# Forty-eight narrow projection columns computed beside the retention's first head of values, in a two-layer trunk kernel

## The chip, the cores and the metric

The kernel runs on one core of a Trainium2 chip. The metric is the device time of one execution in microseconds (us), and lower is better. The engines are called by the profile's names: PE multiplies matrices (PEld is its weight load, which runs beside the multiplication), DVE is the vector engine, ACT the scalar engine, POOL the general one, and SP issues every DMA of this kernel. TensorE's clock has two levels, 1.2 and 2.4 GHz; the profile gives what was granted as a share of the full one.

## What is computed

Two layers of a hybrid trunk over 256 context tokens and 512 latent tokens, 1024 wide. Each layer projects the modulated tokens `h` by one wide matrix `w_in` whose columns are split among three groups of heads:

```python
h_l = x * (1 + sc_l) + sh_l
h_c = cx * (1 + sc_c) + sh_c
parts_l = jnp.split(h_l @ w_in, in_splits(), axis=-1)
parts_c = jnp.split(h_c @ w_in, in_splits(), axis=-1)
ssd_l, ssd_c = ssd_mixer(parts_c[0:3], parts_l[0:3], ...)       # z 1024, xbc 1536, dt 16 columns
mla_l, mla_c = mla_mixer(parts_c[3:7], parts_l[3:7], ...)       # q 384, kv 256, kr 32, gate 512
ret_l, ret_c = retention_mixer(parts_c[7:11], parts_l[7:11], ...)  # q 256, k 256, v 512, gate 512
```

Two of these parts are narrow: `dt` (16 columns, the step sizes of the state-space scan) and `kr` (32 columns, the shared rotary key of the attention). The retention's values `v` are 512 columns in four heads of 128. The outputs of the three mixers are concatenated, projected back, and normalised with the residual.

## The kernel before

All 768 tokens are held on chip with features on the partitions: `hh[k]` and `hl[k]` (k = 0 to 7) are the 128-feature slices of `h`, as a high and a low part in the format fp32r. Every projection is made of triples (`mm3`, line 145): high by high, high by low and low by high. The weights come from HBM in slots (`wslot`, line 153): one DMA into `wr` (two buffers), a cast on ACT into `wh` and a subtraction on DVE into `wl` (three buffers each). A projection result lies in one of three PSUM buffers, `acc`.

There are two ways of projecting.

**Feature-major** (`proj_many`, line 175): the weights are the stationary operand, 128 output columns wide, and the tokens stream past: 512 latent ones, then 256 of context, for each of 8 slices and 3 terms. A tile of 128 columns costs 24 multiplications with 512 moving columns and 24 with 256. The tile `M_T` with the 48 columns of `kr` and `dt` is made in the same way, with a stationary operand 48 wide.

**Token-major** (`ret_v`, line 669): for the values `v`, 128 tokens are the stationary operand and the weights stream past, 256 columns (two heads) at a time: 2 passes over 6 token chunks with 24 multiplications each. The mean of each head is taken off on the way out (DVE reduces into `vm`, ACT adds it into `stv`), and a DMA stores the chunk (`rv`).

The order of the work comes from a list of steps for each layer:

```python
STEPS = ("dt0 xbc0 ssd0 rk0 rq0 rk1 mod0 ckv0 xbc1 rv0 ssd1 rq1 ckv1 cq0 cq2 rg0 rg1 rg2 cq1 rg3 g1 g0",
         "dt0 xbc0 rk1 ssd0 rk0 xbc1 rv0 ssd1 ckv1 ckv0 cq0 cq1 rg0 rg1 rg2 rg3 cq2 g0 g1 g2 g3")
```

A scheduler turns this into one fixed order for each engine before the run, and mixes independent steps; `high_priority` moves a step ahead. Each engine then works through its own list in order.

In layer 0 the opening (`start`, line 316) makes three projection tiles slice by slice while the modulation is still being computed from DMAs: `M_T`, `B_T` and `B_T + 2`. The next step, `dt0` (`dt_stage`, line 439), copies them out, transposes the 48 rows back to token-major (line 470), and computes from `dt` the decay terms that the scan needs, ending with a store of `cum` that is read back later as `cf`. In layer 1 `dt_stage` first projects three other tiles for the latent tokens alone, then `M_T` and `B_T`. The step `xbc0` (line 559) takes the convolution (`conv`, line 539) of `B_T`, `B_T + 2` and four tiles from `X_T` on, on DVE, with padded copies in three buffers `xpad`. At the very end `ln_turned` (line 1265) writes the second half of the output from buffers `ho`, which share two slots with `hr`.

Of the kernel before, what the change touches and what calls it, by code (L numbers as in the profile page):

```python
# [9 lines left out]
F32 = mybir.dt.float32  # L10
F32R = mybir.dt.float32r
I32 = mybir.dt.int32
AF = mybir.ActivationFunctionType
ALU = mybir.AluOpType
AX = mybir.AxisListType
# [3 lines left out]
KD = 8  # L19
NCTX = 256  # L20
NLAT = 512
T = NCTX + NLAT
NCH = T // 128
# [9 lines left out]
XC = 772  # L33
# [9 lines left out]
Z_T, X_T, B_T, Q_T, KV_T, G_T, RQ_T, RK_T, RG_T, RV_T, M_T, NWIN = (  # L43
    0, 8, 16, 20, 23, 25, 29, 31, 33, 37, 41, 42)
# [44 lines left out]
class Trunk:  # L89
# [225 lines left out]

    def start(self, P):

        tiles = ((M_T, 48), (B_T, 128), (B_T + 2, 128))
        lat = [self.acc.tile([128, 512], F32, tag="acc", name="p0") for _ in tiles]
        cx = [self.ps("cx", "c0", 3) for _ in tiles]  # L320
        ws = []
        for k in range(KD):
            for j in (0, 1) if k == 0 else (k + 1,):
                if j < KD:
                    self.ada(0, (j, j + 8), P)
            self.make_h0(P, k)
            if not ws:
                for t, m in tiles:
                    ws.append([x[:, :8 * m].rearrange("p (k c) -> p k c", k=8)
                               for x in self.wslot(self.A["win"][0, t][:, :8 * m], 8 * m)])  # L330
            for ps, a, b in ((lat, NCTX, T), (cx, 0, NCTX)):
                for p, (hi, lo), (t, m) in zip(ps, ws, tiles):
                    self.mm3(p[:m, 0:b - a], [(hi[:, k, :], lo[:, k, :], self.hh[k][:, a:b], self.hl[k][:, a:b])],
                             k == 0, k == KD - 1)
        self.first = []
        for pl, pc, (t, m) in zip(lat, cx, tiles):
            st = self.sp.tile([128, T], F32, tag="st", name="c0s", bufs=3)
            self.copy(st[:m, 0:NCTX], pc[:m, 0:NCTX])
            self.first.append([(pl[:m], NCTX, T), (st[:m, 0:NCTX], 0, NCTX)])
# [75 lines left out]
    def step(self, s):  # L415

        l, D, ctx, n, i = self.l, self.D, self.ctx, s[:-1], int(s[-1])
        if n == "dt":
            self.dt_stage()
        elif n == "xbc":  # L420
            self.xbc(i)
        elif n == "ssd":
            self.ssd(i)
        elif n == "rv":
            self.ret_v()
        elif n == "mod":
            self.pending = [(0, (j, j + 1)) for j in range(16, 24, 2)] + [(1, (j, j + 1)) for j in range(0, 24, 2)]
        else:
            t = dict(rq=RQ_T, rk=RK_T, ckv=KV_T, cq=Q_T, rg=RG_T, g=G_T)[n]
            self.spill(l, t + i, D[n][i], gate=n in ("rg", "g"), ctx=ctx or n in ("rk", "ckv"))  # L430
# [8 lines left out]
    def dt_stage(self):  # L439
        nc, S, l, D = self.nc, self.S, self.l, self.D  # L440
# [6 lines left out]
            nc.vector.memset(xp[:, 774:776], 0.0)  # L447
        self.cnt = 0
        if l == 0:
            first = self.first  # L450
        else:
            rq0, rq1, pc2 = self.proj_lat(l, (RQ_T, RQ_T + 1, B_T + 2))
            self.store(D["rq"][0], rq0)
            self.store(D["rq"][1], rq1)
            self.padded = {B_T + 2: self.pad(pc2)}
            first = self.proj_many(l, [(M_T, 48), (B_T, 128)]) + [None]
        self.pre = {B_T: first[1], B_T + 2: first[2]}
        ms = S.tile([48, T], F32, tag="u", name="ms", bufs=2)
        for p, a, b in first[0]:
            self.copy(ms[:, a:b], p)  # L460
        if l == 0:
            self.padded = {}
        for t in (B_T, B_T + 2):
            if t not in self.padded:
                self.padded[t] = self.pad(self.pre[t])
        self.load(D["kr"], ms[0:32, :])
        pt = self.ps("tr", "pt", 2)
        ptv = pt[:, 0:288].rearrange("p (c h) -> p c h", c=NCH)
        for c in range(NCH):
            nc.tensor.transpose(ptv[:, c, :], ms[:, c * 128:(c + 1) * 128], self.ident[:48, :48])  # L470
        n = 2 * NCH * 16
        mk = lambda nm: S.tile([128, 2, NCH, 16], F32, name=nm)
        fl = lambda t: t.rearrange("p d c h -> p (d c h)")
        x, e, s, q = mk("dtx"), mk("dte"), mk("dts"), mk("dtq")
        for d in range(2):
            self.tt(x[:, d], ptv[:, :, 32:48],
                    pc[:, P_DT + 16 * d:P_DT + 16 * d + 16].unsqueeze(1).to_broadcast([128, NCH, 16]), ALU.add)
        self.ts(fl(e), fl(x), -1.0, ALU.mult)
        self.tt(fl(e), fl(e), fl(x), ALU.min)
# [19 lines left out]
        h = NCH * 16  # L499
# [17 lines left out]
        for d, m in ((0, self.mf), (1, self.mb)):  # L517
            pa = self.ps("tr", "pa", 2)
            pb = self.ps("tr", "pb", 2)
            for c in range(NCH):  # L520
                o = pa[0:16, c * 128:(c + 1) * 128] if c < 4 else pb[0:16, (c - 4) * 128:(c - 3) * 128]
# [144 lines left out]
        self.load(D["y"][g][:, :, c * 128:(c + 1) * 128].rearrange("t p i -> p t i"), ys)  # L666


    def ret_v(self):
        l = self.l  # L670
        for n in range(2):
            sl = [self.wslot(self.A["win"][l, RV_T + n * 2 + j]) for j in range(2)]
            sl = [(a.rearrange("p (k c) -> p k c", k=4), b.rearrange("p (k c) -> p k c", k=4)) for a, b in sl]
            for c in range(NCH):
                p = self.acc.tile([128, 512], F32, tag="acc", name="pv")
                cs = slice(c * 128, (c + 1) * 128)
                self.mm3(p[:, 0:256], [(self.hh[k][:, cs], self.hl[k][:, cs], sl[k // 4][0][:, k % 4, :],
                                        sl[k // 4][1][:, k % 4, :]) for k in range(KD)])
                with self.tc.high_priority():
                    st = self.sp.tile([128, 256], F32, tag="stv", name="stv", bufs=2)  # L680

                    vm = self.sp.tile([128, 2], F32, tag="vm", name="vm", bufs=2)
                    self.nc.vector.tensor_reduce(vm, p[:, 0:256].rearrange("p (h e) -> p h e", e=128), axis=AX.X,
                                                 op=ALU.add, negate=True)
                    self.ts(vm, vm, 1.0 / 128, ALU.mult)
                    for h in range(2):
                        self.act(st[:, h * 128:h * 128 + 128], p[:, h * 128:h * 128 + 128], AF.Identity,
                                 bias=vm[:, h:h + 1])
                    self.load(self.D["rv"][:, c, n * 256:(n + 1) * 256], st)


    def blocks(self):
# [572 lines left out]
    def ln_turned(self, P, X, a, b, qsum, xsum):  # L1265


        pc = self.pc[self.l]
        k = (b - a) // 128
        dg, lgr, lbr = self.turn  # L1270
        po = {}
        for f in range(2):
            for c in range(k):
                po[c, f] = (self.acc.tile([128, 512], F32, tag="acc", name="pot") if f or c else
                            self.ps("pot", "pot", 1))
                for t in range(4):
                    self.mm(po[c, f][:, t * 128:(t + 1) * 128], X[4 * f + t][:, c * 128:(c + 1) * 128], dg[:, 4 * f + t],
                            t == 0, False, skip_group_check=True)
        with self.tc.high_priority():
            pd = self.ps("plm", "pld", 2)  # L1280
            self.mm(pd[0:1, 0:b - a], self.selD[:, 0:1], xsum)
            nd = P.tile([1, 256], F32, name="nd")
            self.act(nd[:, 0:b - a], pd[0:1, 0:b - a], AF.Copy, scale=-1.0)
            v = self.variance(P, qsum, xsum, k)
            y = self.rpow(P, v, k)
        for f in range(2):
            fs = slice(512 * f, 512 * f + 512)
            for c in range(k):
                self.mm(po[c, f], nd[:, c * 128:(c + 1) * 128], lgr[:, fs], False, True, skip_group_check=True)
                o = P.tile([128, 512], F32, tag="hr", name="ho", bufs=2)  # L1290
                self.stt(o, po[c, f], y[:, c:c + 1], lbr[:, fs], ALU.mult, ALU.add)
                self.load(self.out[1][c * 128:(c + 1) * 128, fs], o)

# [55 lines left out]
def kmajor(w, c):  # L1349

    k = w.shape[0] // 128
    return np.ascontiguousarray(w.reshape(k, 128, c).transpose(1, 0, 2)).reshape(128, k * c)


def pack(inputs):
    f = {k: np.asarray(v) for k, v in inputs.items()}
    o = {}
# [3 lines left out]
    w = f["w_ada"].reshape(L, 8, 128, 24, 128)  # L1361
    o["wada"] = w.transpose(0, 3, 2, 1, 4).reshape(L, 24, 128, 1024)
    win = f["w_in"]
# [4 lines left out]
    W = np.zeros((L, NWIN, 128, 1024), win.dtype)  # L1368
    for l in range(L):
        for i, s in enumerate(starts):  # L1370
            W[l, i] = kmajor(win[l, :, s:s + 128], 128)
        for n in range(2):
            for j in range(2):
                W[l, RV_T + n * 2 + j] = kmajor(win[l, j * 512:(j + 1) * 512, 4272 + n * 256:4272 + (n + 1) * 256], 256)
        m = np.concatenate([win[l, :, 3216:3248], win[l, :, 2560:2576]], 1)
        W[l, M_T, :, :384] = kmajor(m, 48)
    o["win"] = W
    uq = f["mla_w_uq"].reshape(L, 384, 8, 96)
    cols = np.concatenate([uq[..., :64].reshape(L, 384, 512), uq[..., 64:].reshape(L, 384, 256)], -1)
# [59 lines left out]
```

## Time and profile before

| | |
|---|---|
| median of 3 runs | 1487.1 us (1483.25 to 1488.01) |
| the profiled execution's own time | 1483.76 us |
| its span, first to last instruction | 1481.8 us |
| PE busy | 1426.5 us, 96% |
| PEld busy | 1158.2 us, 78% |
| DVE busy | 1076.6 us, 73% |
| ACT busy | 692.6 us, 47% |
| mean granted TensorE clock | 0.987 |

The sums of the prediction are made against the profiled execution, 3.3 us below the median of the runs. A busy PE is not a PE at its peak: the recorded length of a multiplication includes its way through the array, so the distance between the starts of two neighbours tells what one costs in a stream.

### The profile page before, as it was taken

The numbers are of one execution on the slowest core, as the hardware profiler recorded it, in microseconds if no ns is written. First come the engines' busy times: TensorE is split into PE (matmuls) and PEld (weight loads), VectorE is DVE, ScalarE is ACT, GpSimd is POOL, SyncE is SP. The second block draws the span as 40 slices with busy tenths as digits, with TensorE's granted clock in tenths as the row PEclk, the third lists the DMA queues.
The fourth block names the chain that finished last, engine by engine and source line by source line (L and its number), as shares of the span: only waits on it lengthen the run. The fifth ranks groups of instructions, "written<-read, shape, count | busy, mean of one in ns | idle before, by whom it ended". The sixth has DMA issues, their size and how long they took to land. (4 is left out here: it accounts for less than half of the span.)

```text
span 1481.8 us, 23394 instructions
## 1 busy us (share of the span) xinstructions
PE 1426.5 (96%) x8696; PEld 1158.2 (78%) x8696; DVE 1076.6 (73%) x2077; ACT 692.6 (47%) x1377; POOL 25.7 (2%) x35
## 2 busy tenths in 40 slices
PE   6999999999999999999999899999999999989988
PEld 4787789778888888777788778788778887767667
DVE  3599894995486667678645858997776767678846
ACT  2346743662232443477622345565463344347742
POOL 0000000000000001000001000000000000100010
PEclk9999999999999999999999999999999999999999
DMA  8336553457725746624241223353357465562241
GB/s 337 138 99 180 183 168 110 158 184 256 258 72 175 247 154 198 222 82 131 80 170 58 91 88 111 120 148 114 98 168 251 136 199 190 171 205 89 69 141 57
DMA packets 109725, 226.18 MB, mean 153 GB/s; under 512 B 13534, under 2 KB 41310, under 8 KB 109356
## 3 DMA queue, kind: packets, MB, share of 16 engines
q1 hardware_dynamic: 109612, 224.70, 46.5%
q8 instruction: 68, 1.11, 0.3%
q14 instruction: 45, 0.37, 0.1%
HBM read 174.46 MB, written 50.20 MB: 152 GB/s over the span
## 5 line engine op out<-in xcount | busy, mean ns | idle before, releaser
L101 PE MATMUL pj<-hh,wh 128*128 128x512 f32 (+1 forms) x984 | 354.5, 361 | 2.8 <-ACT hh L115 2.4
L101 PE MATMUL pj<-hh,wl 128*128 128x512 f32 (+1 forms) x984 | 353.2, 359 | 0.0
L101 PE MATMUL pj<-hl,wh 128*128 128x512 f32 (+1 forms) x984 | 350.7, 356 | 0.0
L122 ACT CAST wh<-wr 128x1024 fp32r<-128x1024 f32 (+1 forms) x116 | 120.3, 1039 | 208.8 <-PE pj L101 92.2
L101 PEld LDWEIGHTS pj<-hh,wh 128*128 128x128 f32 x984 | 185.1, 188 | 36.0 <-issue 8.9
L101 PEld LDWEIGHTS pj<-hh,wl 128*128 128x128 f32 x984 | 185.0, 188 | 31.2 <-issue 7.0
L101 PEld LDWEIGHTS pj<-hl,wh 128*128 128x128 f32 x984 | 185.2, 188 | 30.5 <-issue 6.4
L104 DVE TENSOR_TENSOR wl<-wr,wh 128x1024 fp32r<-128x1024 f32 (+1 forms) x116 | 141.0, 1216 | 79.6 <-ACT wh L122 78.5
L104 DVE TENSOR_TENSOR pel<-pe,peh 128x512 fp32r<-128x512 f32 (+1 forms) x112 | 71.6, 648 | 37.0 <-ACT peh L115 36.5
L107 DVE SCALAR_TENSOR_TENSOR cv<-xpad,cw,cv 128x772 f32<-128x772 f32 (+1 forms) x96 | 92.2, 993 | 0.2
L115 ACT ACTIVATE pe<-psc 128x512 f32<-128x512 f32 (+1 forms) x112 | 63.7, 569 | 56.4 <-PE psc L101 47.6
L1043 DVE TENSOR_REDUCE nm<-pmx 128x1 fp32r<-128x768 f32 (+1 forms) x80 | 67.6, 845 | 15.7 <-PE pmx L101 14.5
L101 PE MATMUL po<-sh,wh 128*128 128x512 f32 (+1 forms) x192 | 70.0, 367 | 4.2 <-DVE oy L107 4.2
L101 PE MATMUL po<-sl,wh 128*128 128x512 f32 (+1 forms) x192 | 70.1, 366 | 1.9 <-DVE sl L107 1.9
L115 ACT ACTIVATE ce<-cf 64x512 f32<-64x512 f32 (+1 forms) x80 | 46.9, 587 | 50.3 <-DMA cf<-cum 49.5
L101 PE MATMUL po<-sh,wl 128*128 128x512 f32 (+1 forms) x192 | 69.6, 364 | 0.0
L115 ACT ACTIVATE tm<-sf,dt 128x128 f32<-128x128 f32 x160 | 52.5, 390 | 30.4 <-DVE sf L104 30.3
L115 ACT ACTIVATE peh<-psc 128x512 fp32r<-128x512 f32 (+1 forms) x112 | 63.6, 568 | 0.2
L101 PE MATMUL po<-mr,wh 128*128 128x256 f32 (+1 forms) x216 | 55.5, 343 | 3.1 <-DVE la L107 3.1
L115 ACT ACTIVATE arg<-arg,ncb 128x128 f32<-128x128 f32 x160 | 54.9, 393 | 4.1 <-DVE arg L107 3.6
L101 PE MATMUL pv<-wl,hh 128*128 128x256 f32 x192 | 54.0, 281 | 0.7 <-DVE wl L104 0.7
L101 PE MATMUL pv<-wh,hh 128*128 128x256 f32 x192 | 53.7, 280 | 0.0
(337 smaller groups left out, 2952.1 us busy)
## 6 DMA issues: line engine op xcount, KB each, us to landing
wr<-in_win SPq DMA_DIRECT2D x82, 512.0 KB, 3.8
ar<-in_wada SPq DMA_DIRECT2D x48, 512.0 KB, 7.0
cf<-cum SPq DMA_DIRECT2D x80, 256.0 KB, 4.6
wr<-in_wout SPq DMA_DIRECT2D x32, 512.0 KB, 4.3
y<-ys SPq DMA_DIRECT2D x20, 256.0 KB, 2.5
xs<-th SPq DMA_DIRECT2D x16, 256.0 KB, 2.1
x<-in_xT SPq DMA_DIRECT2D x8, 384.0 KB, 8.6
rv<-stv SPq DMA_DIRECT2D x24, 128.0 KB, 3.0
```

The source lines that it names most:

```text
L101: return self.nc.tensor.matmul(out, lhsT=lhsT, rhs=rhs, start=start, stop=stop, **k)
L104: return self.nc.vector.tensor_tensor(out, a, b, op=op)
L107: return self.nc.vector.scalar_tensor_tensor(out, in0=a, scalar=s, in1=b, op0=op0, op1=op1)
L115: return self.nc.scalar.activation(out, in_, f, **k)
L122: self.nc.scalar.copy(hi, raw)
L1043: nc.vector.tensor_reduce(nm[:, i:i + 1], p1[:, 0:n], axis=AX.X, op=ALU.max, negate=True)
```

## The change

The tile `M_T` goes. Its 48 columns are laid behind the 128 columns of the retention's first head, and are computed token-major with it. `ret_v` becomes a function of a part number and is called three times for a layer: part 0 with 128 + 48 = 176 moving columns, inside `dt_stage`; part 1 with 256 and part 2 with 128 columns where `rv0` stands in the list. Each part has 6 chunks of 24 multiplications. The `dt` columns are then token-major already; the 32 `kr` columns are transposed instead. In the opening, the place of `M_T` is taken by `X_T`, a full tile of 128 columns, whose projection in `xbc0` goes. The weights are packed anew on the host. The buffers `ho` get four slots of their own.

```diff
     def start(self, P):
-        tiles = ((M_T, 48), (B_T, 128), (B_T + 2, 128))
+        tiles = ((X_T, 128), (B_T, 128), (B_T + 2, 128))
...
         elif n == "rv":
-            self.ret_v()
+            self.ret_v(1)
+            self.ret_v(2)
...
         if l == 0:
-            first = self.first
+            self.padded = {t: self.pad(p) for t, p in zip((B_T, B_T + 2, X_T), (self.first[1], self.first[2], self.first[0]))}
         else:
...
-            first = self.proj_many(l, [(M_T, 48), (B_T, 128)]) + [None]
-        self.pre = {B_T: first[1], B_T + 2: first[2]}
-        ms = S.tile([48, T], F32, tag="u", name="ms", bufs=2)
-        for p, a, b in first[0]:
-            self.copy(ms[:, a:b], p)
-        if l == 0:
-            self.padded = {}
-        for t in (B_T, B_T + 2):
-            if t not in self.padded:
-                self.padded[t] = self.pad(self.pre[t])
-        self.load(D["kr"], ms[0:32, :])
-        pt = self.ps("tr", "pt", 2)
-        ptv = pt[:, 0:288].rearrange("p (c h) -> p c h", c=NCH)
-        for c in range(NCH):
-            nc.tensor.transpose(ptv[:, c, :], ms[:, c * 128:(c + 1) * 128], self.ident[:48, :48])
+
+        mt = S.tile([128, XC], F32, tag="u", name="mt", bufs=2)[:, 0:NCH * 48].rearrange("p (c m) -> p c m", c=NCH)
+        self.ret_v(0, mt)
+        if l:
+            self.padded[B_T] = self.pad(self.proj(l, B_T))
+        kt = S.tile([32, T], F32, tag="u", name="kt", bufs=2)
+        for a, b in ((2, 6), (0, 2)):
+            pt = self.ps("tr", "pt", 2)
+            for c in range(a, b):
+                nc.tensor.transpose(pt[0:32, (c - a) * 128:(c - a + 1) * 128], mt[:, c, 0:32], self.ident)
+            self.copy(kt[:, a * 128:b * 128], pt[0:32, 0:(b - a) * 128])
+        self.load(D["kr"], kt)
...
-            self.tt(x[:, d], ptv[:, :, 32:48],
+            self.tt(x[:, d], mt[:, :, 32:48],
...
-    def ret_v(self):
+    def ret_v(self, n, mt=None):
+
         l = self.l
-        for n in range(2):
-            sl = [self.wslot(self.A["win"][l, RV_T + n * 2 + j]) for j in range(2)]
...
+        h0, nh = ((0, 1), (1, 2), (3, 1))[n]
+        w = 128 * nh + (48 if n == 0 else 0)
+        if n < 2:
+            sl = [self.wslot(self.A["win"][l, RV_T + 2 * n + j][:, 0:4 * w], 4 * w) for j in range(2)]
+            sl = [[x[:, 0:4 * w].rearrange("p (k c) -> p k c", k=4) for x in y] for y in sl]
+        else:
+            x = [y.rearrange("p (k c) -> p k c", k=8) for y in self.wslot(self.A["win"][l, M_T])]
+            sl = [[y[:, 0:4] for y in x], [y[:, 4:8] for y in x]]
+        for c in (2, 3, 4, 5, 0, 1):
+            p = self.acc.tile([128, 512], F32, tag="acc", name="pv")
+            cs = slice(c * 128, (c + 1) * 128)
+            self.mm3(p[:, 0:w], [(self.hh[k][:, cs], self.hl[k][:, cs], sl[k // 4][0][:, k % 4, :],
+                                  sl[k // 4][1][:, k % 4, :]) for k in range(KD)])
+            with self.tc.high_priority():
+                if n == 0:
+                    self.copy(mt[:, c], p[:, 128:176])
...
+                self.load(self.D["rv"][:, c, h0 * 128:(h0 + nh) * 128], st[:, 0:128 * nh])
...
-                o = P.tile([128, 512], F32, tag="hr", name="ho", bufs=2)
+                o = P.tile([128, 512], F32, tag="ho", name="ho", bufs=4)
```

## Rows read from the trace of the kernel before

**Rows 1.** The page: busy time, share of the span and instructions of each engine.
```profile
PE 1426.5 (96%) x8696; PEld 1158.2 (78%) x8696; DVE 1076.6 (73%) x2077; ACT 692.6 (47%) x1377; POOL 25.7 (2%) x35
```

**Rows 2.** Busy time by stretch: stretch, length, engines with counts, clock, DMA.
```profile
core 0: us, PE busy (x) PEld busy (x) DVE busy (x) ACT busy (x) POOL busy (x), PEclk, DMA share, GB/s
20.00:40.00 20.00, 18.45 (x194) 13.31 (x194) 9.30 (x19) 4.13 (x7) 0.00 (x0) 1.00 1.02 405
...
58.00:70.00 12.00, 11.62 (x59) 9.83 (x59) 10.31 (x23) 4.15 (x6) 0.00 (x0) 0.86 0.45 141
...
90.00:222.00 132.00, 130.70 (x883) 106.96 (x883) 124.84 (x242) 79.83 (x190) 0.00 (x0) 1.00 0.52 163
222.00:270.00 48.00, 45.57 (x349) 42.17 (x348) 26.90 (x52) 18.99 (x46) 0.00 (x0) 1.00 0.36 114
...
1010.00:1050.00 40.00, 38.46 (x315) 37.13 (x315) 24.89 (x46) 19.84 (x44) 0.00 (x0) 1.00 0.36 116
```

**Rows 3.** One tile's stretch: multiplications into `pv`, columns PE, PEld, DVE, ACT.
```profile
1034.00:1046.00 12.00, 12.00 (x104) 12.00 (x103) 2.01 (x5) 3.13 (x10) 1.00 0.43 138
```

**Rows 4.** Timeline of PE, layer 1, `M_T`: start, length, engine, instruction.
```profile
860.47 0.39 PE L101 MATMUL pj<-hh,wh 128*48 128x512 f32 x1
...
865.08 0.39 PE L101 MATMUL pj<-hh,wl 128*48 128x512 f32 x1
...
870.90 0.28 PE L101 MATMUL pj<-hh,wh 128*48 128x256 f32 x1
...
873.59 0.28 PE L101 MATMUL pj<-hh,wl 128*48 128x256 f32 x1
```

**Rows 5.** Groups by shape, PE: rows*columns of weights, moving shape, count | busy, mean ns.
```profile
L101 PE MATMUL pv<-wh,hh 128*128 128x256 f32 x192 | 53.7, 280 | 0.0
...
L580 PE MATMUL ptr<-K,th 128*128 128x128 f32 x96 | 13.4, 276 | 3.7 <-DVE th L107 3.6
...
L101 PE MATMUL pnm<-identr,nm 128*1 128x128 f32 x80 | 8.7, 222 | 2.3 <-ACT bqh L118 1.6 <-DVE nm L1043 0.5
...
L470 PE MATMUL pt<-K,ms 48*128 48x48 f32 x12 | 1.1, 228 | 1.6 <-ACT ms L118 1.6
```

**Rows 6.** Timeline: a run of four `pnm` multiplications.
```profile
608.64 0.40 PE L101 MATMUL pnm<-identr,nm 128*1 128x128 f32 x4 [1.47 <-ACT bqh L118]
```

**Rows 7.** Groups by shape, PEld: weight loads of 128, 48 and 1 columns.
```profile
L101 PEld LDWEIGHTS pv<-wl,hh 128*128 128x128 f32 x192 | 36.1, 188 | 0.9 <-DVE wl L104 0.9
...
L101 PEld LDWEIGHTS prc<-ones,rsq 128*128 128x128 f32 x80 | 9.7, 191 | 1.0 <-ACT rsq L115 0.3
...
L101 PEld LDWEIGHTS pnm<-identr,nm 128*1 128x1 f32 x80 | 5.1, 82 | 6.6 <-ACT bqh L118 3.2 <-DVE nm L1043 0.7 <-issue 0.7
...
L101 PEld LDWEIGHTS pj<-hl,wh 128*48 128x48 f32 x16 | 1.9, 121 | 0.9
```

**Rows 8.** Timeline of PEld: weight loads for multiplications with one moving column.
```profile
433.62 0.97 PEld L101 LDWEIGHTS prc<-ones,rsq 128*128 128x128 f32 x8
...
448.12 1.90 PEld L101 LDWEIGHTS prc<-ones,rsq 128*128 128x128 f32 x16
```

**Rows 9.** Timeline: the weights' low part on DVE in the opening.
```profile
14.59 0.55 DVE L104 TENSOR_TENSOR wl<-wr,wh 128x384 fp32r<-128x384 f32 x1
...
16.52 1.23 DVE L104 TENSOR_TENSOR wl<-wr,wh 128x1024 fp32r<-128x1024 f32 x1
```

**Rows 10.** Timeline: PE behind the opening.
```profile
57.85 0.57 PE L470 MATMUL pt<-K,ms 48*128 48x48 f32 x6 [1.60 <-ACT ms L118]
...
60.35 0.63 PE L101 MATMUL pj<-hl,wh 128*128 128x512 f32 x1
```

**Rows 11.** Groups by shape, DVE: the reduction of a chunk of `pv`.
```profile
L683 DVE TENSOR_REDUCE vm<-pv 128x2 f32<-128x256 f32 x24 | 10.1, 422 | 22.6 <-PE pv L101 22.4
```

**Rows 12.** Timeline: the last two output pieces.
```profile
1477.15 1.56 DVE L107 SCALAR_TENSOR_TENSOR ho<-pot,rp_y,lbr 128x512 f32<-128x512 f32 x2 [1.33 <-DMA out<-ho]
```

More of the change, by code (lines that the diff above doesn't have):

```diff
@@ L666, in ssd_y @@
         self.load(D["y"][g][:, :, c * 128:(c + 1) * 128].rearrange("t p i -> p t i"), ys)
-    def ret_v(self):
+    def ret_v(self, n, mt=None):
         l = self.l
-        for n in range(2):
-            sl = [self.wslot(self.A["win"][l, RV_T + n * 2 + j]) for j in range(2)]
[L673 to L689, printed above, removed]
@@ new lines, in ret_v @@
+        h0, nh = ((0, 1), (1, 2), (3, 1))[n]
[14 more added lines that the diff above has]
+                    self.copy(mt[:, c], p[:, 128:176])
+                st = self.sp.tile([128, 256], F32, tag="stv", name="stv", bufs=2)
+                vm = self.sp.tile([128, 2], F32, tag="vm", name="vm", bufs=2)
+                self.nc.vector.tensor_reduce(vm[:, 0:nh], p[:, 0:128 * nh].rearrange("p (h e) -> p h e", e=128),
+                                             axis=AX.X, op=ALU.add, negate=True)
+                self.ts(vm[:, 0:nh], vm[:, 0:nh], 1.0 / 128, ALU.mult)
+                for h in range(nh):
+                    self.act(st[:, h * 128:h * 128 + 128], p[:, h * 128:h * 128 + 128], AF.Identity,
+                             bias=vm[:, h:h + 1])
+                self.load(self.D["rv"][:, c, h0 * 128:(h0 + nh) * 128], st[:, 0:128 * nh])
@@ L1371, in pack @@
             W[l, i] = kmajor(win[l, :, s:s + 128], 128)
[L1372 to L1376, printed above, removed]
+        v = win[l, :, 4272:4784]
+        m = np.concatenate([v[:, 0:128], win[l, :, 3216:3248], win[l, :, 2560:2576]], 1)
+        for j in range(2):
+            W[l, RV_T + j, :, :704] = kmajor(m[j * 512:(j + 1) * 512], 176)
+            W[l, RV_T + 2 + j] = kmajor(v[j * 512:(j + 1) * 512, 128:384], 256)
+        W[l, M_T] = kmajor(v[:, 384:512], 128)
     o["win"] = W
```

## The prediction, made before the changed kernel had run

> **What bounds the kernel now.** I read the page first. PE is busy for 96% of the span, the next engine, DVE, for 73% [rows 1]: what counts is how long PE's list is, unless the change opens a hole in it. Then the busy time by stretch. Behind the opening, from 90 to 222 us, PE (130.7 of 132 us) and DVE (124.8) are both nearly full; in the two stretches that hold the values' projection, 222 to 270 and 1010 to 1050, DVE has room (26.9 of 48 us, 24.9 of 40) and PE loses 2.4 and 1.5 us [rows 2]. So PE sets the time there too, and a longer list of PE moves the end by about as much.
>
> The third reading is the pace, because a recorded length (280 ns for 256 columns, 222 for 128) holds the way through the array as well [rows 5]. In a stream of `pv`, 104 multiplications of 256 columns take 12.00 us, one in 115.4 ns [rows 3]. In `M_T`, 512 columns follow each other in 4.61 us over 20 steps, 230.5 ns, and 256 columns in 2.69 us over 23 steps, 117 ns [rows 4]. That is 0.45 ns a moving column, whether the weights are 48 or 128 wide.
>
> **The term that decides: 176 and 128 moving columns.** No fp32r multiplication of this kernel has a stationary operand of 128 columns and fewer than 256 moving ones, so its cost must be bounded. Two things could set the pace: the moving columns, or the load of the next weights.
>
> From below, the moving columns. `pnm` is fp32r with 128 moving columns and a stationary operand of one column: four take 0.40 us, so (0.40 - 0.222) / 3 = 59 ns each [rows 5, 6]. The narrow format therefore pays no penalty of its own at 128 columns, and 176 would be 81 ns in proportion.
>
> From above, the load. A load of 1, 48 and 128 columns is recorded with 82, 121 and 188 ns [rows 7]. From 1 to 128 columns that is 106 ns more, 0.83 ns a column, and the 48 lie on the same line (82 + 39 = 121): 82 ns of delay, then 107 ns in which 128 columns go in. If the array takes in one set of weights at a time, two such loads can't start within 107 ns. The trace has one place that shows this: `prc`, weights of 128 columns with one moving column. Eight loads take 0.97 us and sixteen 1.90 us, so (0.97 - 0.191) / 7 = 111 ns and (1.90 - 0.191) / 15 = 114 ns a step [rows 7, 8], with next to nothing to stream. `pnm`, with one column of weights, shows that PE can step in 59 ns, so the 111 ns are those of the load.
>
> With 256 moving columns the load hides behind the stream (107 under 115). With 176 or 128 it would stand out, and both would cost some 112 ns, almost as much as 256. I take 112 (between the 111 and 114 of `prc`, whose loads are almost as long as those of `pv`, 191 and 188 ns); the bounds are 107 and 117 if the load binds, and 59 and 81 ns if it doesn't.
>
> The sum for a layer. Before: 288 multiplications of `pv` at 0.1154 = 33.2 us, and for `M_T` 24 at 0.2305 and 24 at 0.117 = 8.3 us; 41.6 us together. After: 3 parts of 144; part 1 at 0.1154 = 16.6 us, parts 0 and 2 at 0.112 = 32.3 us; 48.9 us. That is 7.3 us more a layer, **+14.6 us** for both; +11.7 at 107 ns, +17.4 at 117, and -9.6 if only columns count (16.6 + 144 x (0.059 + 0.081) = 36.8 us a layer). In columns the change saves 11,520 of 92,160 a layer, but it issues 432 multiplications for 336, and each brings a load.
>
> The Trainium skill (TensorE: Matmul & The Clock Gate, "Back-to-back issue gap") speaks for the change: it gives a sustained 81 ns for a pair of load and multiplication at 128 columns and 131 ns at 512. The second doesn't agree with this trace, which has 230 ns at 512 columns. By 81 ns for both narrow kinds the sum would be 23.3 + 16.6 = 39.9 us a layer, 3.4 us less in all, where my 112 ns gives 14.6 more.
>
> **The other parts.**
> - Projection of `X_T` in the opening instead of in `xbc0`: the same 48 multiplications with the same moving columns. The weight slot grows from 384 to 1024 columns, which is 320 KB more in a stretch where the DMA engines are full at 405 GB/s [rows 2]: at most 0.8 us. On DVE its low part takes 1.23 instead of 0.55 us [rows 9], before PE's first products. I take +0.5 us, between 0 and 1.
> - Transposes: 12 of the kind of `pt` (228 ns) become 12 with 128 moving columns, like `ptr` (276 ns) [rows 5]: 12 x 0.048 = +0.6 us, at least 0.
> - The pass out of PSUM: 18 chunks a layer are reduced instead of 12, at no more than 0.42 us each [rows 11], with six more small scalings, copies and stores of `rv` on DVE, ACT and SP. For parts 1 and 2 DVE's room in [rows 2] hides it, and with 3 PSUM buffers at 24 x 112 ns = 2.7 us a chunk PE has 5 us before it would miss a buffer. Without that cover, 6 x 0.42 = 2.5 us a layer would stand on the path. I take 0. SP gets 6 more issues a layer; behind them stand weight loads that have a slot of slack.
> - The chain from `dt` to `cum`: in layer 0 it now waits for part 0, some 16 us of PE, instead of standing right behind the opening. What is late is `cum`, and behind it `cf` and the scan. The scan also needs the four convolved tiles of `X`, though, and DVE can begin on three convolutions while PE makes part 0. In layer 1 part 0 (16 us) stands where `M_T` and `B_T` stood (together some 16 us), so `dt` is no later and `B_T` comes 8 us later.
> - The hole behind the opening: PE waits 1.6 us for copies of `ms`, and works on at half pace (0.63 instead of 0.40 us recorded) under a granted clock of 0.86 [rows 2, 10]. The next weights are cast behind the same number of copies on ACT, so this hole stays, without the wait for the transposes. With convolutions begun earlier, some of the 2.4 and 1.5 us of [rows 2] may go as well. I take -1.2 us, bounds -5 and +3.
> - Four slots for `ho`: DVE waited 1.33 us for a store before the third piece [rows 12], but that piece also needs PE's last products. I take -0.5 us, between -1.3 and 0.
>
> Sum: 14.6 + 0.5 + 0.6 - 1.2 - 0.5 = **+14.0 us**. The profiled execution's 1483.8 becomes 1497.8; beside the median of the runs, 3.3 us above it, this is 1501.
>
> **The rivals.**
> 1. *The load doesn't bind.* If two loads may run side by side in this form, the moving columns count: -9.6 + 0.5 + 0.6 - 1.2 - 0.5 = -10.2 us, 1477. (The Trainium skill's page named above would have it at 81 ns: -3.4 - 0.6 us, 1483.) For it: the 48-wide and 128-wide weights show the same pace at 256 columns, so no load has been seen to cost there. Against it: `prc`. It decides as soon as the narrow pace is under some 87 ns, where 288 x pace + 16.6 us equals the 41.6 us of before.
> 2. *The holes pay for it.* The load binds at its lower bound, +11.7, and the holes behind the opening and in the values' stretches close altogether, some 8 us, with the earlier convolutions: about +3 us, 1490, not to be told from no change. Against it: DVE has no room from 90 to 222 us, and what it gains there must first be met by PE's work.
> 3. *The late chain hurts as well.* `cum` comes 16 us later in layer 0 and the tiles of `X` 8 us later in layer 1; if the scan waits for either, PE runs out of other work, and 5 to 8 us come on top: 1508. Against it: PE has the other projections of the list to fill in.
>
> **How the numbers follow.** The forecast, a load-bound pace and slower by 9 to 20 us, gets 0.72; rival 1 0.15; rival 2 0.08; rival 3 0.05. About 0.3% (4.5 us) is what the runs can tell from no change. Faster: rival 1 in most of its reach and a little of rival 2, 0.16. Same: most of rival 2 and the edge of rival 1, 0.09. Slower: 0.75. The forecast's own range is 1494 to 1508. The 8-in-10 range takes in rivals 2 and 3 and the slower edge of rival 1: 1483 to 1511.
>
> **What would show it.** In the changed kernel's rows: the distance between starts in `pv` with 176 and 128 columns, 107 to 117 ns if I am right, near 81 and 59 if rival 1 is; the busy time of PE, up by about 14 us, with PEld nearly as full as PE in the three parts; PE's idle time behind the opening still near 2 us; `dt`'s first operation in layer 0 some 16 us later, and DVE busy with `cv` before it. I am wrong if the narrow multiplications step faster than some 87 ns, or if PE's idle time, not its list, moved the end.

## The result, and the profile after

The changed kernel takes 1521.6 us in the median (1521.2 to 1525.2) against 1485.8 for the kernel before in the same comparison: 1.0246, 95% interval 1.0222 to 1.0269, or 36 us more. The prediction was slower by 14 us, within 1483 to 1511: the sign was right, the size well below half. The span grew from 1481.8 to 1519.5 us. The page's row of the engines, beside [rows 1], and its row of the granted clock in 40 slices:

```profile
PE 1460.7 (96%) x8888; PEld 1193.8 (79%) x8888; DVE 1081.0 (71%) x2101; ACT 694.2 (46%) x1389; POOL 25.7 (2%) x35
...
PEclk9779999999999999999999899999999999999999
```

PE is busy for 34.2 us more and idle for 3.5 us more: its busy time grew, as forecast, but more than twice as much. How much of that is a longer list, and how much the clock, is worked out below. Two slices near the start stand at 7, where no slice of the kernel before was under 9. Three stretches of `pv` show why (as in [rows 2], and to be read beside the pace of [rows 3]): part 0 of layer 0, part 0 of layer 1, part 2 of layer 1.

```profile
62.00:88.00 26.00, 26.00 (x124) 26.00 (x124) 3.36 (x11) 3.87 (x11) 0.00 (x0) 0.50 0.20 66
893.00:905.00 12.00, 12.00 (x110) 12.00 (x109) 5.12 (x26) 4.81 (x14) 0.00 (x0) 1.00 0.41 133
1075.00:1088.00 13.00, 13.00 (x119) 13.00 (x118) 3.25 (x12) 2.35 (x7) 0.00 (x0) 1.00 0.39 118
```

Where the clock is 1.00 (2.4 GHz), 12.00 us hold 110 multiplications and 13.00 us hold 119: 109 ns each, with PEld as full as PE. In layer 0 the granted clock is 0.50 (1.2 GHz) for the whole stretch, and 26.00 us hold only 124: 210 ns. DVE, moreover, does next to nothing there, 3.36 of 26 us. The timeline of PE, for the way into part 0 of layer 0, the way out of it, and the pace in layer 1:

```profile
57.06 0.28 PE L101 MATMUL c<-hh,wl 128*128 128x256 f32 x1
59.34 0.57 PE L101 MATMUL pv<-wh,hh 128*128 128x176 f32 x3 [2.00 <-ACT wh L122]
60.26 0.52 PE L101 MATMUL pv<-wl,hh 128*128 128x176 f32 x1 [0.35 <-DVE wl L104]
...
75.51 0.41 PE L101 MATMUL pv<-wh,hl 128*128 128x176 f32 x1
...
80.63 0.41 PE L101 MATMUL pv<-wh,hl 128*128 128x176 f32 x1
...
91.58 0.78 PE L101 MATMUL pj<-hh,wh 128*128 128x512 f32 x1
...
93.43 0.63 PE L101 MATMUL pj<-hl,wh 128*128 128x512 f32 x1
93.86 0.45 PE L101 MATMUL pj<-hh,wl 128*128 128x512 f32 x1
94.15 0.39 PE L101 MATMUL pj<-hh,wh 128*128 128x512 f32 x1
...
891.50 0.28 PE L101 MATMUL pv<-wh,hh 128*128 128x176 f32 x1
...
897.64 0.28 PE L101 MATMUL pv<-wh,hl 128*128 128x176 f32 x1
```

The last two rows are 55 steps apart: 6.14 / 55 = 111.6 ns. In layer 0 the recorded length goes from 0.28 to 0.41 us behind a hole of 2.00 and 0.35 us, and the rows of 75.51 and 80.63 are 24 steps apart: 5.12 / 24 = 213 ns. It stays so until the projections with 512 moving columns: the one at 93.43 still takes 0.63, the one at 94.15 0.39. In [rows 2, 10] the same fall was made good sooner: a clock of 0.86 over 12 us is 3.4 us at the half level, and such projections stood right behind the hole. Last, DVE: `dt`'s first operation, the first convolution, and the last two output pieces, and behind them the first two of these in the kernel before:

```profile
91.12 0.25 DVE L104 TENSOR_TENSOR dtx<-mt,pc 128x96 f32<-128x96 f32 x1
...
106.65 0.68 DVE L112 TENSOR_SCALAR cv<-xpad,cw 128x772 f32<-128x772 f32 x1 [1.83 <-DMA cum<-ct]
...
1514.11 0.75 DVE L107 SCALAR_TENSOR_TENSOR ho<-pot,rp_y,lbr 128x512 f32<-128x512 f32 x1
1515.82 0.75 DVE L107 SCALAR_TENSOR_TENSOR ho<-pot,rp_y,lbr 128x512 f32<-128x512 f32 x1 [0.96 <-PE pot L101]
```

```profile
58.46 0.42 DVE L104 TENSOR_TENSOR dtx<-pt,pc 128x96 f32<-128x96 f32 x2 [4.66 <-PE pt L470]
...
75.79 0.69 DVE L112 TENSOR_SCALAR cv<-xpad,cw 128x772 f32<-128x772 f32 x1 [2.02 <-ACT ct L118]
```

No convolution runs under part 0. The first one stands behind the whole chain of `dt` and waits at its end for the transfer of `ct`, whose buffers (tag `cv`) are those of the convolutions. In the kernel before it stands in the same place, 31 us earlier.

### The profile page after: what moved, and what is told of

The parts are those of the page before. It is cut to its first block, busy times and chain, and to the rows that moved or that the text cites. A ratio compares the mean times of both kernels' runs of the same rounds, so it can differ in the third digit from the quotient of the medians.

```text
span 1519.5 us, 23852 instructions
## 1 busy us (share of the span) xinstructions
PE 1460.7 (96%) x8888; PEld 1193.8 (79%) x8888; DVE 1081.0 (71%) x2101; ACT 694.2 (46%) x1389; POOL 25.7 (2%) x35
## 5 line engine op out<-in xcount | busy, mean ns | idle before, releaser
L101 PE MATMUL pj<-hh,wh 128*128 128x512 f32 (+1 forms) x952 | 342.0, 360 | 4.2 <-ACT hh L115 2.4
L101 PE MATMUL pj<-hl,wh 128*128 128x512 f32 (+1 forms) x952 | 342.6, 360 | 0.0
L101 PE MATMUL pj<-hh,wl 128*128 128x512 f32 (+1 forms) x952 | 340.8, 358 | 0.0
L101 PEld LDWEIGHTS pj<-hh,wh 128*128 128x128 f32 x952 | 180.1, 189 | 36.0 <-issue 7.9
L101 PEld LDWEIGHTS pj<-hl,wh 128*128 128x128 f32 x952 | 180.2, 189 | 29.8 <-issue 7.2
L101 PEld LDWEIGHTS pj<-hh,wl 128*128 128x128 f32 x952 | 180.3, 189 | 28.7 <-issue 6.1
L101 PE MATMUL pv<-wh,hh 128*128 128x176 f32 (+2 forms) x288 | 86.0, 300 | 2.1 <-ACT wh L122 2.0
L101 PE MATMUL pv<-wl,hh 128*128 128x176 f32 (+2 forms) x288 | 86.4, 300 | 0.4 <-DVE wl L104 0.4
L101 PE MATMUL pv<-wh,hl 128*128 128x176 f32 (+2 forms) x288 | 86.5, 300 | 0.0
L101 PEld LDWEIGHTS pv<-wh,hh 128*128 128x128 f32 x288 | 61.1, 213 | 3.1 <-ACT wh L122 2.6
```

The source lines that it names most:

```text
L101: return self.nc.tensor.matmul(out, lhsT=lhsT, rhs=rhs, start=start, stop=stop, **k)
```

## The experiments

Three accounts were to be told apart. **Pace and clock:** the load holds narrow multiplications at 112 ns (+14.6 us), and in layer 0 part 0 also runs at half the clock: 144 x (213 - 111.6) ns = +14.6 us. **Late chain:** what comes late on DVE costs the time, whatever the clock. **Pace alone** would leave 20 us without a cause. Ratios are to the kernel before; a difference of 0.001 is 1.5 us.

### A. The load's price by itself: `split3` and `split3b`

Both cut one of the two passes of values of the kernel *before* into two of 128 columns, in both layers; nothing else changes. `split3` cuts the first pass of `rv0`:

```
+            for h0, nh in ((0, 1), (1, 1)) if n == 0 else ((0, 2),):      # split3b: n == 1
+                for c in range(NCH):
...
+                    ws = slice(h0 * 128, (h0 + nh) * 128)
+                    self.mm3(p[:, 0:128 * nh], [(self.hh[k][:, cs], self.hl[k][:, cs], sl[k // 4][0][:, k % 4, ws],
+                                                 sl[k // 4][1][:, k % 4, ws]) for k in range(KD)])
...
```

> The kernel before, with only the first pass of ret_v cut into two passes of one head (128 columns): 432 multiplications a layer for 288, the same columns in all, M_T and the opening untouched. It runs in the stretch of rv0, where PE has the full clock. If the load of 128 weight columns binds (111.5 ns a step at 128 columns): 288 x 0.1115 + 144 x 0.1154 = 48.7 us a layer for 33.2, so +15.5 us a layer and about +31 us in all, with 111 to 112 ns between starts. If only the columns count (59 ns at 128 columns): the time stays within 0.3%. If the +36 us of the changed kernel come from the late chain to cum and an idle VectorE rather than from the pace: also near no change, since dt and cum stand where they stood.

Measured: 1.0622 (1.0588 to 1.0655), +93 us, three times the expectation. Windows of `pv` (columns PE alone), and the timeline of PE: the hole, and the change from 128 to 256 columns:

```profile
core 0: us, PE busy (x), PEclk, DMA share, GB/s
255.00:285.00 30.00, 30.00 (x143) 0.50 0.05 14
290.00:295.00 5.00, 5.00 (x29) 0.60 0.63 224
295.00:300.00 5.00, 5.00 (x45) 1.00 0.15 52
```

```profile
234.18 1.54 PE L580 MATMUL ptr<-K,th 128*128 128x128 f32 x6 [6.40 <-DVE th L107]
...
288.96 0.41 PE L101 MATMUL pv<-wh,hl 128*128 128x128 f32 x1
289.17 0.52 PE L101 MATMUL pv<-wh,hh 128*128 128x256 f32 x1
...
293.76 0.41 PE L101 MATMUL pv<-wh,hh 128*128 128x256 f32 x1
293.97 0.32 PE L101 MATMUL pv<-wl,hh 128*128 128x256 f32 x1
294.13 0.28 PE L101 MATMUL pv<-wh,hl 128*128 128x256 f32 x1
```

PE waited 6.40 us for a convolution soon after the pass began, the clock fell, and 30 us in which PE was never idle show 0.50 and 210 ns a step. The pass of 256 columns that follows without a gap starts at 0.21 us a step as well, and from 293.97 on, 4.8 us later, runs at the full level. So what brought the level back was the wider stream. The second layer repeats it, with 3.5 us. `split3b` has the same multiplications with the wide pass first:

> split3 with the other pass of the values cut: the pass of 256 columns goes first in rv0, so that the convolutions' waits fall into it, and the 288 multiplications of 128 columns follow it without a hole. If a hole and narrow columns together are needed to keep the clock low: granted clock 1.00 in the narrow stretch, 111 to 112 ns a step, +15.5 us a layer, so about +31 us on the kernel before (1519) and some 60 less than split3. If a long load-bound stream lowers the clock by itself: again some 210 ns a step and near 1580.

Measured: 1.0237 (1.0198 to 1.0277), +35 us. Windows of `pv`: the hole's place, just behind it (both in the wide pass), and the narrow stretch:

```profile
235.00:240.00 5.00, 4.07 (x21) 0.66 0.37 131
240.00:244.00 4.00, 4.00 (x36) 1.00 0.11 36
252.00:272.00 20.00, 20.00 (x182) 1.00 0.14 45
```

In layer 0 the clock fell here too, but in the wide pass, which brought it back; in layer 1 it didn't fall. The narrow stretch then steps in 20.00 / 182 = 110 ns, and holds the full level for as long as it lasts. The price is confirmed (31 expected, 35 with an interval of 29 to 41). That it is the load which sets it, and not another limit of each multiplication with 128 weight columns, still rests on `pnm` and `prc` [rows 6, 8], since no run changed the weights' width. The 58 us between the two kernels are the order of the passes, with the hole that falls into one or the other.

### B. The clock in part 0: `warm` and `pad256`

`warm` takes the step `rk0` of layer 0 (512 and 256 columns) out of `STEPS[0]` and puts it ahead of part 0; `pad256` fills part 0 with 80 columns of zeros, in both layers:

```
+        if l == 0:
+            self.step("rk0")
         self.ret_v(0, mt)
...                                   # above warm, below pad256
-        w = 128 * nh + (48 if n == 0 else 0)
+        w = 256 if n == 0 else 128 * nh
```

> The changed kernel, with the projection rk0 (48 multiplications of 512 and 256 columns) of layer 0 moved ahead of part 0. Theory 1 (part 0 of layer 0 ran at the 1.2 GHz level because nothing with wide columns stood between the hole behind the opening and it): the granted clock in part 0 is near 1.00, its steps some 112 ns instead of 213, and the kernel gets some 15 us faster than the changed one, about 1506 us. Rival (the chain from dt to cum, late by part 0, starves the scan): dt comes as late or later, the kernel stays at 1520 or gets up to 8 us slower, whatever the clock.

> The changed kernel, with part 0 padded from 176 to 256 moving columns by 80 columns of zeros (both layers); number of multiplications, loads and order stay. At full clock that costs 144 x (0.1154 - 0.1116) = 0.5 us a layer. If it is the narrow columns that leave the clock at 1.2 GHz behind the opening, the clock comes back early in part 0 of layer 0 and the kernel is some 10 to 15 us faster than the changed one (1507 to 1512). If the load-bound stream as such doesn't bring the clock back, or the hole ahead of it sets the clock, part 0 stays at some 210 ns a step and the time is 1521 to 1523.

Measured: `warm` 1.0120 (1.0094 to 1.0147), `pad256` 1.0138 (1.0116 to 1.0160), 19 and 16 us under the changed kernel's 1.0246. Windows of `pv` in part 0 of layer 0, of `warm` and then of `pad256`:

```profile
66.00:80.00 14.00, 12.50 (x113) 12.62 (x113) 1.17 (x4) 2.27 (x8) 1.00 0.31 106
```

```profile
60.00:74.00 14.00, 14.00 (x122) 14.00 (x121) 1.46 (x5) 2.84 (x10) 1.00 0.41 129
```

Both are at 1.00, with 111 and 115 ns. Columns of zeros, which compute nothing, made the kernel 16 us faster. In both a part 0 that is shorter also lets `dt` begin earlier (84.7 and 76.5 us for 91.12), and in `pad256` PE then waits 4.08 us for an `xpad` buffer at 98.8, 1.77 in the changed kernel, so the gains hold other things as well; what the clock costs by itself is in the steps, 213 for 111 ns. "No gain", the rival's word for `warm`, is out. But in both the level never fell behind the opening, and a 256-column pass in the same place did see it fall (`late`, below). So these two runs price the level; that a wider stream brings it back is shown by `split3` and `late`.

### C. The late chain: `late`, `ahead`, `ahead2`

`late` moves, in the kernel before, the first pass of values of layer 0 (256 columns) to the place of part 0:

```
+        if l == 0:
+            self.ret_v((0,))
...
         pt = self.ps("tr", "pt", 2)
...                                   # rv0 of layer 0 keeps the second pass alone
```

> The kernel before with its first pass of values (256 moving columns, 144 multiplications) in layer 0 moved from rv0 to the place of part 0: behind the opening, ahead of the transposes of ms, so ahead of dt. Same instructions, only their order. If the late chain from dt to cum costs time of its own beside pace and clock: dt's first operation in layer 0 some 17 us later, the first pst that much later, and at the end of layer 0 and of the program 5 to 9 us more than before. If the lateness is made up by PE's other projections, as the prediction had it: within 0.3% of before.

Measured: 1.0019 (1.0004 to 1.0033), +2.8 us: inside the 0.3% of the second branch, with an interval that just passes it. The six transposes of `ms` kept their place ahead of the pass, so `dt` began at 58.94 and only what comes behind PE's next step was late: the first convolution at 88.13 against 75.79. The run prices 12 us of lateness, not the 31 us of the changed kernel.

The same run is the plainest control for the clock. In the place of part 0, with waits of PE of 1.60, 0.38 and 0.58 us in front, it has 144 multiplications of 256 columns. The level fell, with steps of 0.21 us, and came back under these multiplications some 7 us later; 176 columns in that place didn't bring it back in 31 us:

```profile
60.00:70.00 10.00, 9.45 (x57) 9.46 (x58) 7.28 (x17) 2.51 (x7) 0.00 (x0) 0.67 0.45 130
70.00:80.00 10.00, 10.00 (x88) 10.00 (x87) 4.66 (x16) 3.15 (x9) 0.00 (x0) 1.00 0.26 95
```

`ahead` is the changed kernel with the convolutions of B and C of layer 0 in front of part 0; `ahead2` has them in `ret_v(0)`, behind the casts of its weights:

```
+        self.cw = ...              # both: cw, uB and uC move here from further down
...
         self.ret_v(0, mt)          # ahead: conv(B_T), conv(B_T + 2) in front of this line
...
         for c in (2, 3, 4, 5, 0, 1):
+            # ahead2: in front of this loop, if n == 0 and l == 0
+            self.conv(B_T, self.uB)
+            self.conv(B_T + 2, self.uC)
```

> The changed kernel, with the two convolutions of B and C of layer 0 put ahead of part 0 in DVE's order (ct no longer ahead of them in the buffers of cv). If DVE's idle time under part 0 (25 of 32 us) is what the late chain costs: 6 to 9 us faster than the changed kernel, 1513 to 1516, with the granted clock in part 0 still near 0.50 and some 213 ns a step. If DVE's idle time is free, or if the reductions of part 0 behind the convolutions hold PE up for buffers: 1520 or more.

> ahead again, with the two convolutions of layer 0 behind the casts of part 0's weights, so that PE doesn't wait 5.6 us for them between 60 and 70 us. Part 0 still runs at the 1.2 GHz level, and DVE convolves under it. If the late convolutions are a part of the 36 us of the changed kernel: 6 to 9 us faster than it, 1513 to 1516. If they are not: within 0.3% of it, 1517 to 1526.

Measured: `ahead` 1.0231 (1.0216 to 1.0245), `ahead2` 1.0174 (1.0142 to 1.0207). One window, 60 to 70 us, of `ahead` and then of `ahead2`:

```profile
60.00:70.00 10.00, 4.39 (x20) 4.39 (x21) 9.13 (x11) 2.74 (x3) 0.00 (x0) 0.50 0.23 74
```

```profile
60.00:70.00 10.00, 10.00 (x49) 10.00 (x49) 9.13 (x12) 3.19 (x6) 0.00 (x0) 0.50 0.48 165
```

DVE is busy for 9.13 us in both, mostly with convolutions. In `ahead` the low parts of the weights stood behind those convolutions on DVE, and PE lost 5.6 us in the window; what was gained was given back. Without that hole the new order is worth 0.0072, some 11 us (5 to 17 with both intervals; 9.1 by the spans), at an unchanged clock of 0.50 in part 0. So the order of the convolutions costs something. How much isn't shown. The page of `ahead2` has

```profile
PE 1451.4 (96%) x8888; PEld 1189.1 (79%) x8888; DVE 1081.1 (72%) x2101; ACT 695.4 (46%) x1389; POOL 25.7 (2%) x35
```

and PE's timeline in the changed kernel, where the late convolutions hold it up:

```profile
112.70 0.38 PE L101 MATMUL pj<-hh,wh 128*128 128x256 f32 x1 [1.77 <-ACT xpad L118]
```

PE is idle for 59.0 of 1510.4 us in `ahead2`, and for 58.8 of 1519.5 in the changed kernel. The wait of 1.77 us is gone, but all of the 9.1 us lie in its busy time, with the same 8888 multiplications. Some 2 us of them come from the opening, ahead of every convolution (PE is busy for 37.33 us from 15 to 57 us, at a clock of 1.00; 39.48 at 0.96 in the changed kernel). The mean granted clock of the whole is 0.980 for 0.976: some 12 us less at the half level, or 6 us of time (an estimate from these two numbers), the opening included. What lowered the clock at the other places, and whether the late convolutions had a part in it, is open. Whether the order on DVE or the buffers shared with `ct` made them late wasn't separated.

### D. Fewer loads: `wide2` and what follows from it

Values and the 48 columns in two passes instead of three, 304 and 256 columns, so 288 multiplications a layer:

```
-        h0, nh = ((0, 1), (1, 2), (3, 1))[n]
+        h0, nh = ((0, 2), (2, 2))[n]
```

> The changed kernel, with the values and the 48 columns in two passes instead of three: 304 columns (two heads and the 48) and 256 columns, 288 multiplications a layer, in the places of part 0 and of rv0. At the full clock 144 x (304 x 0.45 + 115.4) ns = 36.4 us a layer against 48.9 for the three parts and 41.6 for the kernel before. If the pace of the load is what the three parts cost, the kernel is some 25 us faster than the changed one, or 40 if the clock comes back as well: 1481 to 1496. Rival (the late chain to cum sets the +36): part 0 at 304 columns ends later than at 176, and the time stays above 1510.

> wide2 with the projection rk0 of layer 0 ahead of the pass of 304 columns. If the 2.4 GHz level through the opening's end is worth something and the later dt isn't: 2 to 4 us under wide2, 1484 to 1487. If each us that dt is later comes back as a wait for DVE's convolutions: no gain or up to 5 us slower.

Measured: 1.0001 (0.9982 to 1.0019), 36 us under the changed kernel, and 1.0000 (0.9984 to 1.0016) with `rk0` in front, no gain. In `wide2` the fall behind the opening is made good inside the part (0.50 at 62 to 64 us, 1.00 at 66 to 78). Against the kernel before, 10 us should have been won. The timeline of PE in `wide2` has a part of the loss:

```profile
102.03 0.40 PE L101 MATMUL pj<-hh,wl 128*128 128x512 f32 x1
106.91 0.58 PE L101 MATMUL pj<-hh,wh 128*128 128x256 f32 x1 [4.49 <-ACT xpad L118]
```

`pj` has to leave PSUM for an `xpad`, of which there are three, and these are held by convolutions that haven't been made. Three kernels move the convolutions, in both layers (in layer 1 the projection of B goes ahead of the pass too): `wide2_conv` as in `ahead`, `wide2_c2` as in `ahead2`, `wide2_c1` with B's alone.

> wide2 (passes of 304 and 256 columns) with the convolutions of B and C put ahead of the first pass in DVE's order, in both layers; in layer 1 the projection of B goes ahead of the pass as well. wide2 should have gained 10 us on the kernel before by its multiplications and gained none. If the idle DVE took those 10 us: 5 to 10 us faster than before, 1477 to 1482. If not: within 0.3% of wide2, or slower where the reductions behind the convolutions hold up PE's buffers.

> wide2_conv with the two convolutions put behind the casts of the pass's weights instead of ahead of them, so that the hole of 6.4 us of PE that wide2_conv opened at 60 to 70 us closes and DVE still convolves under the first pass. If late convolutions are what ate wide2's 10 us: the wait of PE for xpad at 102 us (4.49 us in wide2) is gone and the time is 1478 to 1484, faster than before by 0.3 to 0.7%. If the 10 us go elsewhere: within 0.3% of before again.

> As wide2_c2, with the convolution of B alone under the first pass, so that the reductions of the pass stand behind 5.7 us of DVE less. If DVE's convolutions hold up the reductions and so PE's three buffers in wide2_c2, this is the faster of the two, by 1 to 3 us; if only the amount of DVE work done under the pass counts, it is 2 to 4 us slower than wide2_c2.

Measured: `wide2_conv` 1.0002 (0.9991 to 1.0014), `wide2_c2` 0.9961 (0.9947 to 0.9976), `wide2_c1` 0.9945 (0.9929 to 0.9962). Windows of `wide2_conv`, then two of `wide2_c2`:

```profile
60.00:70.00 10.00, 3.64 (x13) 3.35 (x14) 10.00 (x12) 2.39 (x3) 0.00 (x0) 0.50 0.10 31
```

```profile
60.00:70.00 10.00, 9.36 (x50) 9.04 (x49) 8.17 (x10) 1.61 (x4) 0.00 (x0) 0.69 0.47 138
...
100.00:110.00 10.00, 10.00 (x57) 8.55 (x57) 8.59 (x10) 5.10 (x10) 0.00 (x0) 1.00 0.45 111
```

`wide2_conv` only moved the hole forward (6.4 us lost at 60 to 70). With the casts first, PE is full from 100 to 110 and the kernel is 6 us faster than the one before, 8 us with B's convolution alone. These two beat both kernels. Which of them is better isn't told by intervals that overlap. Here the late convolutions do show as a wait: PE's idle time over the whole span is 66.0 us in `wide2` (in an execution 4 us above its median), 60.1 in `wide2_c2` and 58.7 in `wide2_c1`.

## Why the prediction was too small

- **The term that decides** held at the full clock: 111.6 ns at 176 columns and 112 at 128 (six steps in 0.67 us at 1075.5), where 112 was taken from `prc` [rows 7, 8]; rival 1 with 59 and 81 ns is out. Its 14.6 us are in the 36. The rule of the Trainium skill that the prediction weighed (TensorE: Matmul & The Clock Gate, "Back-to-back issue gap", 81 ns at 128 columns) doesn't agree with these rows.
- **The step that failed** is part 0 of layer 0 in that sum: "parts 0 and 2 at 0.112" was applied to a place where the prediction itself had read a granted clock of 0.86 and half pace behind the hole. It said that "this hole stays", and took its price to stay as well. The hole stayed (2.35 us for 1.60), but what stood behind it changed, from 512 moving columns to 176, and the half level lasted over 30 us instead of 3.4. That is the missing 14.6 us: 213 instead of 111.6 ns for 144 multiplications; `warm` and `pad256` won back as much and a little more, with `dt` earlier too.
- **The second step that failed:** "DVE can begin on three convolutions while PE makes part 0". It began on none: 106.65 us instead of 75.79, and `dt` at 91.12 instead of 58.46, twice as late as forecast, because part 0 took twice as long. The listing could have told: in `dt_stage` `ct` takes both buffers of the tag `cv` ahead of the first convolution. `ahead2` puts at most some 11 us on this, and the trace of the changed kernel shows only 1.77 us of it as a wait of PE. Rival 3 had the right direction (5 to 8 us on top), but by the wait for `cum`; what the run moved were the convolutions.
- **Opening** +0.5: the last product of the opening ends some 1.1 us later (59.34 - 2.00 against 57.85 - 1.60 of [rows 10]), but that is the clock and not the larger slot: the two rows below are the same opening in the changed kernel and in `pad256`, where PE needs 2.2 us less at 1.00 for 0.96 and ends at 55.2. So the term itself came out at nothing or below. **`ho`** -0.5: the wait of 1.33 us for the store [rows 12] is gone, 0.96 us for PE's last products took its place; right. **Holes** -1.2: wrong in sign, since PE's idle time grew by 3.5 us in all. Rival 2 falls with it.

```profile
15.00:57.00 42.00, 39.48 (x347) 31.09 (x348) 19.57 (x48) 12.00 (x21) 0.00 (x0) 0.96 0.66 253
```

```profile
15.00:57.00 42.00, 37.24 (x348) 29.71 (x348) 19.62 (x48) 13.98 (x26) 0.00 (x0) 1.00 0.69 261
```

The 37.7 us between the spans can be divided without the experiments. The granted clock stands at 0.50 or at 1.00, so a mean of 0.976 over 1519.5 us is some 73 us at the half level, and 0.987 over 1481.8 us some 39. The 34 us more cost about 17 us, if PE is busy in them (an estimate): 14.6 in part 0, the rest in the opening and in places that weren't looked into. That leaves 17 of the 34.2 us of busy time for a longer list, where the prediction had 14.6 + 0.5 + 0.6, and 3.5 us are PE's idle time. So the load and the clock of part 0 carry 29 of 37.7, and the late convolutions have a share in the other 8.5 that the runs don't separate. `ahead2` agrees: with the load and the clock of part 0 unchanged, 26 us (21 to 31) over the kernel before are left.

## What to carry to other kernels

Price a moved stream with the clock of its new place: look up what the granted clock was there, which instructions brought it back, and whether the new ones can. When columns are cut out of a matrix multiplication whose stationary operand is 128 columns wide, count loads, not columns; adding 48 columns to a pass of 256 was cheaper than any narrower pass. When work of another engine is pulled forward, keep it behind that engine's part in feeding PE, or the gain comes back as a hole (`ahead` and `ahead2`, `wide2_conv` and `wide2_c2`).

## What was unexpected of the hardware

PE was busy without a break for 30 us with 128 moving columns, weights loading all the time, and the granted clock stayed at 0.50; 256 moving columns behind them, at the same 0.21 us a step, ended that. In `late` 256 columns ended it in the very place where 176 didn't. The other way round it isn't symmetric: in `split3b` 20 us of the same narrow multiplications kept a clock of 1.00 that they had been given. At 0.50 the step was 0.21 us with 128, 176 and 256 columns alike. What decides whether a hole of some 2 us lowers the clock stays open: in the changed kernel 2.35 us behind the opening did, in `pad256` 2.27 and 0.64 us didn't.
